# Summing modulation vectors over the partitions: a GpSimd reduction and an accumulating DMA in place of TensorE

## The chip, the cores and the metric

The kernel runs on one core of a Trainium2 chip. A core has engines that each work through their own instruction queue and wait for one another by semaphores: TensorE (PE in the profile, with its weight loads as PEld), VectorE (DVE), ScalarE (ACT), GpSimd (POOL) and SyncE (SP), which here issues most of the DMAs. The metric is the device time of one execution in microseconds (us), lower is better.

## The reference, cut to what matters

Two layers work on 256 latent and 256 context tokens of width 1024. Each layer is a half-step FFN, a mixer (neighbourhood attention in layer 0, a short convolution in layer 1) and a second half-step FFN. Around each of them the tokens are scaled, shifted and gated by modulation vectors, nine for each layer (shift, scale and gate for each of the three sub-layers); the context has its own.

```python
def half_step_ffn(x, shift, scale, gate, w_in, w_out, g, b):
    y = swiglu_ffn(modulate(x, shift, scale), w_in, w_out)
    return post_norm_update(x, y, gate, 0.5, g, b)
...
    s_c = jax.nn.silu(c)
    s_cc = jax.nn.silu(c_ctx)
    for i in range(DEPTH):
...
        m = (s_c @ ada_w[i] + ada_b[i]).reshape(B, N_MOD, 1, D)
        mc = (s_cc @ ada_w[i] + ada_b[i]).reshape(N_MOD, D)
```

The change is about the two lines for `m` and `mc`: a vector of 1024 times a matrix of 1024 x 9216, plus a bias. `m[:, 2]` is the gate of the first FFN, `m[:, 3]` and `m[:, 4]` shift and scale of the mixer, and so on.

## The kernel before, in words

**The matmuls.** All operands are float32. For TensorE each is split into a high part in the fp32r format and a low part that holds the rest, and each product is three matmuls: high by high, high by low, low by high. A weight goes this way: SP loads it to a raw tile (`w1r`, `w2r`; L205), ScalarE writes the high part (`w1h`; L210), VectorE subtracts it from the raw tile for the low part (`w1l`; L213, both inputs in SBUF), and TensorE multiplies (L679 in the first FFN, L164, L165 and L167 elsewhere). The activations between the two GEMMs of an FFN are split in the same way: `gh` by ScalarE, `gl` by VectorE (L113), from the gate product `sil` (L689). Every kind of tile has a few buffers, and a load waits until VectorE and ScalarE have read the buffer's last content.

**The first FFN** goes in three parts (`parts`, over the hidden columns). Each part is an input GEMM into `f` and an output GEMM from `gh` and `gl`; the output GEMM's results are multiplied by the gate and added to the tokens.

**The modulation vectors** come in two ways. Shift and scale of the first FFN are computed ahead of it. All other vectors, nineteen of 1024 numbers, come from the background generator `ada` (L275 to L332). The kernel's loops call `tick`, which runs a step of this generator at a given rate (0.45 steps a tick, 0.6 from the third group on), so that its instructions are queued among those of the GEMMs. A group has two vectors (the last has one):

- for each of eight row blocks `k`, SP loads a tile `ar` of 128 x 1024 weights (L303, three buffers), and VectorE multiplies it by column `k` of silu(c) and adds it onto the vector's `acc`, 128 x 1024, in two halves (L294 for the first `k`, a product only; L296 for the others). `acc` has two buffers, one for each vector of a group;
- three steps that issue nothing pass;
- what remains is the sum over the 128 partitions. TensorE multiplies `acc` by a tile of ones (L327, two halves a vector, so four matmuls a group, float32), VectorE adds the bias rows `adab` to the result `ada` in PSUM and writes `adar` (L328), and SP writes that to `scr` in DRAM (L330). The bias rows had been loaded by SP (L318) to a tile that POOL zeroed (L315).

In groups 1 to 3 the two vectors are the latents' and the context's of the same modulation, so they share their `ar` tiles: each tile is added onto both. In the later groups the two vectors have different weights, and the second `acc` is first written when the first one's eight tiles are done.

The first stream (L717) has seven groups and runs from about 80 us to the end of the first FFN. Group 1 makes the gates of the first FFN, which SP loads back from `scr` and broadcasts to all partitions after the first third (L743, `gate`). Groups 2 and 3 make shift and scale of the mixer, which `fold_cols` (L355) loads and transposes. Groups 8 to 10 follow in later phases (L1111, L1114, L1176).

POOL has little else to do: the constants at the start, two tiny operations in each layer norm (`rs`, L402 and L403), and the `bias` of the attention (L883).

Of the kernel before, what the change touches and what calls it, by code (L numbers as in the profile page):

```python
# [8 lines left out]

F32 = mybir.dt.float32  # L10
F32R = mybir.dt.float32r
AF = mybir.ActivationFunctionType
ALU = mybir.AluOpType
# [3 lines left out]
P = 128  # L17
D = 1024
# [52 lines left out]
def backbone_kernel(  # L71
# [6 lines left out]
    nc = tc.nc  # L78
    sync = nc.sync
    cp = ctx.enter_context(tc.tile_pool(name="cp", bufs=1))  # L80
# [7 lines left out]
    hp = phase.__enter__()  # L88
# [6 lines left out]
    def nm(s):  # L95
        uid[0] += 1
        return f"{s}_{uid[0]}"
# [4 lines left out]
    def bank(tag, s):  # L102
        return pp.tile([P, 512], F32, tag=tag, bufs=PB[tag], name=nm(s))
# [4 lines left out]
    def tpb(s="tp"):  # L108
        return bank("tp", s)
# [122 lines left out]

    sm.tile([P, PAD], F32, tag="fill", name="fill")
    win_sb = cp.tile([P, 64], F32, tag="wmask", name="wmask")
    ones = cp.tile([P, 32], F32, tag="ones", name="ones")
# [7 lines left out]
    warm = cp.tile([1, 1], F32, tag="warm", name="warm")  # L243
# [16 lines left out]
    nc.vector.memset(ones, 1.0)  # L260
# [11 lines left out]
    bias_rows = []  # L272
    gate_ins = []

    def ada(vecs):  # L275


        acc = {}

        def accumulate(l, m, k, w):  # L280
            with ExitStack() as st:
                for i in gate_ins:
                    st.enter_context(tc.issue_after(i.ins))
                for i, vec in enumerate(vecs):
                    if vec[:2] != (l, m):
                        continue
                    if k == 0:
                        a = hp.tile([P, D], F32, tag="acc", bufs=2, name=nm("acc"))
                        acc[i] = [a[:, 0:512], a[:, 512:D]]
                    sc = cst[:, k, vec[2]:vec[2] + 1]  # L290
                    for h in range(2):
                        src, a = w[:, h * 512:(h + 1) * 512], acc[i][h]
                        if k == 0:
                            nc.vector.tensor_scalar(a, src, sc, None, op0=ALU.mult)  # L294
                        else:
                            nc.vector.scalar_tensor_tensor(out=a, in0=src, scalar=sc, in1=a,  # L296
                                                           op0=ALU.mult, op1=ALU.add)

        loaded = []
        for l, m in dict.fromkeys((l, m) for l, m, _ in vecs):  # L300
            for k in range(KC):
                w = hp.tile([P, D], F32, tag="ar", bufs=3, name=nm("ar"))
                sync.dma_start(w, ada_w[l, k * P:(k + 1) * P, m * D:(m + 1) * D])  # L303
# [12 lines left out]
        bt = bias_rows[0]  # L316
        for i, (l, m, v) in enumerate(vecs):
            sync.dma_start(bt[64 * i:64 * i + 64:32], ada_b[l, m * D:(m + 1) * D].rearrange("(a b) -> a b", b=512))  # L318
        yield 1
        yield 1  # L320
        yield 1
        rows = hp.tile([P, 512], F32, tag="adar", name=nm("adar"))
        ps = tpb("ada")
        for i in range(len(vecs)):
            for h in range(2):
                j = 2 * i + h
                nc.tensor.matmul(ps[32 * j:32 * j + 32, :], ones, acc[i][h], start=True, stop=True)  # L327
        nc.vector.tensor_tensor(out=rows[:32 * n], in0=ps[:32 * n], in1=bt[:32 * n], op=ALU.add)  # L328
        for i, (l, m, v) in enumerate(vecs):
            sync.dma_start(scr[l][v, m * D:(m + 1) * D].rearrange("(a b) -> a b", b=512),  # L330
                           rows[64 * i:64 * i + 64:32, :])
        yield 1  # L332

    made = [0]

    def stream(*groups):
        for g in groups:
# [130 lines left out]
    def run(gen):  # L468
        for _ in gen:
            pass  # L470
# [555 lines left out]
    hp = phase.__enter__()  # L1026
# [35 lines left out]
    for i in range(len(steps) + LAG + V_LAG):  # L1062
# [14 lines left out]
        n = int(credit)  # L1077
# [12 lines left out]
        j = i - LAG - V_LAG  # L1090
# [14 lines left out]
    hTs, later = box  # L1105
    phase = tc.tile_pool(name="ph2", bufs=1)
    hp = phase.__enter__()
    bias_rows.clear()
# [19 lines left out]
    w = sc_w_in[0]  # L1128
# [45 lines left out]
    g, hTs, later = sub_end(sc_w_out[0], lhs_T(yT), KC, 1, 1, 5, 1.0, (1, 6), "wo", order_late(KU))  # L1174
# [57 lines left out]
```

## Time and profile before

| | |
|---|---|
| time, median of 3 runs | 1262.65 us (1261.54 to 1262.88) |
| span of the profiled execution | 1259.9 us |
| TensorE busy | 1245.4 us, 99% |
| VectorE busy | 952.5 us, 76% |
| ScalarE busy | 589.9 us, 47% |
| GpSimd busy | 41.4 us, 3% |
| HBM read, written | 265.27 MB, 2.17 MB |

The profiled execution has no time of its own beside its span, which lies 2.75 us under the median of the runs. The profile is one execution of the program as the hardware profiler recorded it. A row of a timeline has the start, the duration, the engine, the line, the operation, output<-inputs, and how many instructions are joined in the row; brackets at its end hold the idle time before it and what ended that. Matmuls are pipelined: a duration overlaps the next one's, so what a matmul costs is read from the distance between starts. A row of a group has the count, the busy time, the mean (or the smallest, median and largest) duration in ns, and the idle time of the engine ahead of the group's instructions. A row of the waits reads: waiting engine, line, what it waited for, us in total, times, longest.

### The profile page before, as it was taken

The numbers are of one execution on the slowest core, as the hardware profiler recorded it, in microseconds if no ns is written. First come the engines' busy times: TensorE is split into PE (matmuls) and PEld (weight loads), VectorE is DVE, ScalarE is ACT, GpSimd is POOL, SyncE is SP. The second block draws the span as 40 slices with busy tenths as digits, with TensorE's granted clock in tenths as the row PEclk, the third lists the DMA queues.
The fourth block names the chain that finished last, engine by engine and source line by source line (L and its number), as shares of the span: only waits on it lengthen the run. The fifth ranks groups of instructions, "written<-read, shape, count | busy, mean of one in ns | idle before, by whom it ended". The sixth has DMA issues, their size and how long they took to land.

```text
span 1259.9 us, 17303 instructions
## 1 busy us (share of the span) xinstructions
PE 1245.4 (99%) x5922; PEld 1007.2 (80%) x5922; DVE 952.5 (76%) x1678; ACT 589.9 (47%) x1152; POOL 41.4 (3%) x71
## 2 busy tenths in 40 slices
PE   9999999999999999999999999999999999999997
PEld 6787778777878877877888788888788887888786
DVE  3699987888878877889898546988546788876546
ACT  2432132312326456687655435655435644655431
POOL 0000000000001011121000000000000000000000
PEclk9999999999999999999999999999999999999999
DMA  9976678878842744465899645898645764886641
GB/s 300 310 241 215 197 239 280 269 255 266 300 149 85 217 93 92 93 130 170 256 342 318 225 144 169 285 340 268 214 145 170 247 202 131 262 289 184 223 158 55
DMA packets 202776, 268.59 MB, mean 213 GB/s; under 512 B 30090, under 2 KB 149362, under 8 KB 202688
## 3 DMA queue, kind: packets, MB, share of 16 engines
q1 hardware_dynamic: 202652, 267.48, 67.3%
q8 instruction: 46, 0.75, 0.2%
q14 instruction: 42, 0.34, 0.1%
q10 hardware_dynamic: 36, 0.02, 0.0%
HBM read 265.27 MB, written 2.17 MB: 212 GB/s over the span
## 4 chain that ended last, share of the span: by engine, by line
PE 92%; DVE 3%; ACT 3%; issue 1%; DMA 0%; POOL 0%; DVEq 0%; SPq 0%; ACTq 0%; POOLq 0%
PE f L679 19%; PE w L164 17%; PE w L167 17%; PE w L165 17%; PE wkv L164 2%; PE wkv L165 2%; PE wkv L167 2%; PE wc L164 2%; PE wc L167 2%; PE wc L165 2%; PE gT L487 1%; PE ada L608 1%; PE ada L327 1%; PE S L971 1%; ACT pr L979 1%
## 5 line engine op out<-in xcount | busy, mean ns | idle before, releaser
L210 ACT ACTIVATE w1h<-w1r 128x512 fp32r<-128x512 f32 (+1 forms) x352 | 199.8, 620 | 180.4 <-DMA w1r<-in_ffn_w_in_dram 73.3
L213 DVE TENSOR_TENSOR w1l<-w1r,w1h 128x512 fp32r<-128x512 f32 (+1 forms) x352 | 222.9, 679 | 44.6 <-ACT w1h L210 43.3
L164 PE MATMUL w<-w1h,hTh 128*128 128x512 f32 x528 | 209.4, 397 | 0.9 <-ACT hTh L112 0.9
L165 PE MATMUL w<-w1l,hTh 128*128 128x512 f32 x528 | 206.0, 390 | 0.2 <-DVE w1l L213 0.2
L296 DVE SCALAR_TENSOR_TENSOR acc<-ar,cst,acc 128x512 f32<-128x512 f32 x266 | 186.0, 746 | 15.4 <-DMA ar<-in_ada_w_dram 15.4
L164 PE MATMUL w<-w2h,gh 128*128 128x512 f32 (+1 forms) x446 | 173.4, 389 | 0.0
L165 PE MATMUL w<-w2l,gh 128*128 128x512 f32 (+1 forms) x446 | 172.1, 386 | 0.0
L213 DVE TENSOR_TENSOR w2l<-w2r,w2h 128x512 fp32r<-128x512 f32 x176 | 114.3, 688 | 76.0 <-ACT w2h L210 75.2
L210 ACT ACTIVATE w2h<-w2r 128x512 fp32r<-128x512 f32 x176 | 101.6, 624 | 146.0 <-PE w L167 103.6
L167 PE MATMUL w<-w1h,hTl 128*128 128x512 f32 x528 | 163.2, 390 | 0.3 <-DVE hTl L113 0.2
L167 PE MATMUL w<-w2h,gl 128*128 128x512 f32 (+1 forms) x446 | 136.1, 386 | 0.0
L679 PE MATMUL f<-h0h,w1h 128*128 128x512 f32 x352 | 133.3, 394 | 0.4 <-DVE h0h L634 0.4
L679 PE MATMUL f<-h0l,w1h 128*128 128x512 f32 x352 | 133.2, 391 | 0.0
L679 PE MATMUL f<-h0h,w1l 128*128 128x512 f32 x352 | 132.7, 390 | 0.0
L164 PEld LDWEIGHTS w<-w1h,hTh 128*128 128x128 f32 x528 | 99.2, 188 | 23.8 <-ACT hTh L112 1.7
L167 PEld LDWEIGHTS w<-w1h,hTl 128*128 128x128 f32 x528 | 98.9, 188 | 22.4 <-DVE hTl L113 1.5
L165 PEld LDWEIGHTS w<-w1l,hTh 128*128 128x128 f32 x528 | 99.2, 188 | 20.2 <-DVE w1l L213 0.6
L164 PEld LDWEIGHTS w<-w2h,gh 128*128 128x128 f32 x446 | 83.8, 188 | 19.2 <-issue 1.7
L165 PEld LDWEIGHTS w<-w2l,gh 128*128 128x128 f32 x446 | 83.8, 188 | 16.6
L167 PEld LDWEIGHTS w<-w2h,gl 128*128 128x128 f32 x446 | 83.3, 188 | 17.1
L679 PEld LDWEIGHTS f<-h0h,w1h 128*128 128x128 f32 x352 | 65.9, 189 | 18.8 <-issue 4.2
L679 PEld LDWEIGHTS f<-h0l,w1h 128*128 128x128 f32 x352 | 65.6, 188 | 14.3 <-issue 0.6
(186 smaller groups left out, 1684.5 us busy)
## 6 DMA issues: line engine op xcount, KB each, us to landing
w1r<-in_ffn_w_in_dram SPq DMA_DIRECT2D x340, 256.0 KB
ar<-in_ada_w_dram SPq DMA_DIRECT2D x128, 512.0 KB
w2r<-in_ffn_w_out_dram SPq DMA_DIRECT2D x88, 512.0 KB
ar<-in_ada_w_dram SPq DMA_DIRECT2D x32, 256.0 KB
wkvr<-in_na_w_qkv_dram SPq DMA_DIRECT2D x32, 256.0 KB
wcr<-in_sc_w_in_dram SPq DMA_DIRECT2D x32, 256.0 KB
wqr<-in_na_w_qkv_dram SPq DMA_DIRECT2D x8, 512.0 KB
wor<-in_na_w_out_dram SPq DMA_DIRECT2D x8, 512.0 KB
```

Source lines behind the costliest of these rows:

```text
L164: nc.tensor.matmul(ps, lh, rh, start=first and i == 0, stop=False)
L165: nc.tensor.matmul(ps, lh, rl, start=False, stop=False)
L167: nc.tensor.matmul(ps, ll, rh, start=False, stop=last and i == n - 1)
L210: nc.scalar.activation(hi[:, a:a + m // W_HI], raw[:, a:a + m // W_HI], AF.Copy)
L213: nc.vector.tensor_tensor(out=lo[:, a:b], in0=raw[:, a:b], in1=hi[:, a:b].bitcast(F32), op=ALU.subtract)
L296: nc.vector.scalar_tensor_tensor(out=a, in0=src, scalar=sc, in1=a, op0=ALU.mult, op1=ALU.add)
L327: nc.tensor.matmul(ps[32 * j:32 * j + 32, :], ones, acc[i][h], start=True, stop=True)
L487: nc.tensor.transpose(ps[:, j * 256 + i * P:j * 256 + (i + 1) * P], g[:, j * P:(j + 1) * P], ident)
L608: nc.tensor.matmul(ps[o:o + 32, 0:m], cst[:, a * kt + i, :], w[:, i, j, :], start=(a == 0 and i < 2), stop=(a == last and i >= kt - 2))
L679: nc.tensor.matmul(ps, w, hT0[k][part == 1], start=(k == part == 0), stop=(k == KC - 1 and part == 1))
L971: nc.tensor.matmul(banks[i], (qh, qh, ql)[f][ps, qs], (kh, kl, kh)[f][ps, :], start=f == 0, stop=f == 2)
L979: nc.scalar.activation(pr, S, AF.Exp, bias=mx[:, 0:1], accum_out=mx[:, 1:2])
```

## The change

The multiplication of `ar` by silu(c) and its accumulation on VectorE stay. The sum over the partitions is made by POOL: `partition_all_reduce`, a library instruction, reads `acc` (128 x 1024) and writes the sum to all partitions of a new tile `red`, which has one buffer. A DMA on POOL's queue then adds row 0 of `red` onto `scr` in DRAM. So that the bias is in the sum, three DMAs of SP copy `ada_b` to `scr` beforehand. The tile of ones, the bias rows, the matmuls of L327, the addition of L328 and the writes of L330 are gone. Where a group's end took four steps of the generator, it takes one. After a stream's last reduction a tiny POOL operation on `warm` follows it.

```diff
-                        a = hp.tile([P, D], F32, tag="acc", bufs=2, name=nm("acc"))
-                        acc[i] = [a[:, 0:512], a[:, 512:D]]
+                        acc[i] = hp.tile([P, D], F32, tag="acc", bufs=2, name=nm("acc"))
...
+        def summed(i):
+            l, m, v = vecs[i]
+            red = hp.tile([P, D], F32, tag="red", name=nm("red"))
+            nc.gpsimd.partition_all_reduce(red, acc[i], P, ReduceOp.add)
+            nc.gpsimd.dma_start(scr[l][v:v + 1, m * D:(m + 1) * D], red[0:1], accum_op=ALU.add)
+            if i == len(vecs) - 1 and made[0] + 1 == groups[0]:
+                nc.gpsimd.tensor_tensor(out=warm, in0=red[0:1, 0:1], in1=lnc[0:1, 0:1], op=ALU.add)
...
-        n = 2 * len(vecs)
-        if not bias_rows:
-            bias_rows.append(hp.tile([P, 512], F32, tag="adab", name=nm("adab")))
-            nc.gpsimd.memset(bias_rows[0], 0.0)
-        bt = bias_rows[0]
-        for i, (l, m, v) in enumerate(vecs):
-            sync.dma_start(bt[64 * i:64 * i + 64:32], ada_b[l, m * D:(m + 1) * D].rearrange("(a b) -> a b", b=512))
+        for i in range(len(vecs)):
+            summed(i)
         yield 1
-        yield 1
-        yield 1
-        rows = hp.tile([P, 512], F32, tag="adar", name=nm("adar"))
-        ps = tpb("ada")
-        for i in range(len(vecs)):
-            for h in range(2):
-                j = 2 * i + h
-                nc.tensor.matmul(ps[32 * j:32 * j + 32, :], ones, acc[i][h], start=True, stop=True)
-        nc.vector.tensor_tensor(out=rows[:32 * n], in0=ps[:32 * n], in1=bt[:32 * n], op=ALU.add)
-        for i, (l, m, v) in enumerate(vecs):
-            sync.dma_start(scr[l][v, m * D:(m + 1) * D].rearrange("(a b) -> a b", b=512),
-                           rows[64 * i:64 * i + 64:32, :])
-        yield 1
...
     sync.dma_start(win_sb, win_mask)
+    for l, v in ((0, 0), (0, 1), (1, 0)):
+        sync.dma_start(scr[l][v].rearrange("(a b) -> a b", a=16), ada_b[l].rearrange("(a b) -> a b", a=16))
     sync.dma_start(rope, rope_tab.rearrange("(t p) a b -> p t a b", p=P))
```

The order in which the instructions stand is set by the generator's steps, so it moves as well. In the rows that follow, `acc`, `ar`, `w1r`, `w1h`, `w1l`, `sil`, `f` and `gl` are the tiles named above with the numbers of their buffers; a wait on Pool, PE, DVE or Activation is one on that engine, one on DMAHW is one on a DMA that SP or ACT issued, one on DMASW one that POOL issued. Lines are those of the kernel named: L293 and L291 after the change are L296 and L294 before it, L214 is L213, L678 is L689, L114 is L113, L308 is L303, L734 is L743, L206 is L205.

VectorE, at the border of groups 1 and 2, before the change:

```order
L296 SCALAR_TENSOR_TENSOR acc_711<-ar_897,cst,acc_711 128x512
L296 SCALAR_TENSOR_TENSOR acc_714<-ar_897,cst,acc_714 128x512 [waits DVE_49] x2
L213 TENSOR_TENSOR w1l_1033<-w1r_1031,w1h_1032 128x512 [waits DMAHW7_49,DMAHW2_49]
L213 TENSOR_TENSOR w1l_1042<-w1r_1040,w1h_1041 128x512 [waits DMAHW1_49,DMAHW0_49]
L213 TENSOR_TENSOR w1l_1033<-w1r_1031,w1h_1032 128x512
L213 TENSOR_TENSOR w1l_1042<-w1r_1040,w1h_1041 128x512
L689 TENSOR_TENSOR sil_157_944<-sil_157_944,f_155_915 128x512 [waits PE_49,Activation_49]
L113 TENSOR_TENSOR gl_948<-sil_157_944,gh_947 128x512 [waits Activation_49]
L294 TENSOR_SCALAR acc_994<-ar_992,cst 128x512 [waits DMAHW6_49,PE_49]
L328 TENSOR_TENSOR adar_970<-ada_971,adab_922 128x512 [waits DMAHW4_49,PE_49]
```

VectorE at the same border after the change:

```order
L293 SCALAR_TENSOR_TENSOR acc_712<-ar_898,cst,acc_712 128x512 [waits DVE_49]
L293 SCALAR_TENSOR_TENSOR acc_715<-ar_898,cst,acc_715 128x512 [waits DVE_49] x2
L291 TENSOR_SCALAR acc_943<-ar_941,cst 128x512 [waits DMAHW1_49,Pool_49]
L291 TENSOR_SCALAR acc_943<-ar_941,cst 128x512
L214 TENSOR_TENSOR w1l_1054<-w1r_1052,w1h_1053 128x512 [waits DMAHW5_49,DMAHW3_49]
L293 SCALAR_TENSOR_TENSOR acc_943<-ar_969,cst,acc_943 128x512 [waits DMAHW2_49,DVE_49]
L293 SCALAR_TENSOR_TENSOR acc_943<-ar_969,cst,acc_943 128x512 [waits DVE_49]
L214 TENSOR_TENSOR w1l_1045<-w1r_1043,w1h_1044 128x512 [waits DMAHW4_49]
L214 TENSOR_TENSOR w1l_1054<-w1r_1052,w1h_1053 128x512
L678 TENSOR_TENSOR sil_161_955<-sil_161_955,f_155_916 128x512 [waits PE_49,Activation_49]
L291 TENSOR_SCALAR acc_946<-ar_941,cst 128x512 [waits Pool_49]
```

The next group's first product now stands directly behind the last accumulate of the group before, where six instructions of other work lay between, and it waits for POOL where it waited for TensorE; its second vector's first product waits for POOL again, six rows on. The bias addition is gone.

POOL, from the constants to the second group, before and after. `ISA` is a library load where it has no operands, and the reduction where it has them.

```order
L315 MEMSET adab_922 128x512
masks.py:199 ISA
masks.py:199 AFFINE_SELECT ident<-ident 128x128 [waits Pool_49]
L402 TENSOR_TENSOR rs_3345<-mv_3343,lnc 128x1 [waits DVE_49,Pool_49]
L403 TENSOR_TENSOR rs_3345<-rs_3345,lnc 128x1 [waits Pool_49]
```

And after:

```order
masks.py:199 AFFINE_SELECT ident<-ident 128x128 [waits Pool_49]
L299 ISA
L299 ISA red_923<-acc_712 128x1024 [waits DVE_49]
L300 DMA scr_114<-red_923 16x1x64 [waits DMAHW0_49,Pool_49]
L299 ISA red_926<-acc_715 128x1024 [waits DMASW0_49,DVE_49]
L300 DMA scr_114<-red_926 16x1x64 [waits DMAHW3_49,Pool_49]
L299 ISA red_1155<-acc_943 128x1024 [waits DMASW1_49,DVE_49]
L300 DMA scr_114<-red_1155 16x1x64 [waits Pool_49]
```

Each reduction waits for its `acc` on VectorE and for the landing of the DMA before it, which reads the one buffer of `red`. The `rs` operations come behind the first stream's reductions.

SP, where the first gate is loaded, after the change:

```order
L308 DMA ar_987<-in_ada_w_dram 128x1024 [waits DMAHW6_49,DMAHW3_49,DVE_49]
L734 DMA gate_1136<-scr_114 128x1024 [waits DMAHW4_49,DMASW0_49]
L206 DMA w2r_1175<-in_ffn_w_out_dram 128x2x512 [waits DMAHW5_49,DVE_49,Activation_49]
L308 DMA ar_1006<-in_ada_w_dram 128x1024 [waits DMAHW1_49,DVE_49]
L308 DMA ar_1030<-in_ada_w_dram 128x1024 [waits DMAHW7_49,DMAHW2_49,DVE_49]
```

The two writes of L330 that stood ahead of the gate load are gone; the gate load waits for POOL's first accumulating DMA instead, and a load of `w2r` and further loads of `ar` stand behind it. On TensorE nothing moves but that the 38 `ada` matmuls are gone.

More of the change, by code (lines that the diff above doesn't have):

```diff
@@ L6 @@
 from concourse import mybir
+from concourse.bass_isa import ReduceOp
 from concourse.masks import make_identity
@@ L234, in backbone_kernel @@
     win_sb = cp.tile([P, 64], F32, tag="wmask", name="wmask")
-    ones = cp.tile([P, 32], F32, tag="ones", name="ones")
     ident = cp.tile([P, P], F32, tag="ident", name="ident")
@@ L259, in backbone_kernel @@
     nc.scalar.activation(cst[:, :, 0:2], pt[:, 0:16].rearrange("p (v k) -> p k v", v=2), AF.Silu)
-    nc.vector.memset(ones, 1.0)
     sel = cp.tile([P, 4], F32, tag="sel", name="sel")
@@ L269, in backbone_kernel @@
     xscr = tc.dram_tile([2 * P, D], F32, name="xscr")
-    bias_rows = []
     gate_ins = []
@@ L287, in accumulate @@
                     if k == 0:
-                        a = hp.tile([P, D], F32, tag="acc", bufs=2, name=nm("acc"))
-                        acc[i] = [a[:, 0:512], a[:, 512:D]]
+                        acc[i] = hp.tile([P, D], F32, tag="acc", bufs=2, name=nm("acc"))
                     sc = cst[:, k, vec[2]:vec[2] + 1]
                     for h in range(2):
-                        src, a = w[:, h * 512:(h + 1) * 512], acc[i][h]
+                        src, a = w[:, h * 512:(h + 1) * 512], acc[i][:, h * 512:(h + 1) * 512]
                         if k == 0:
@@ L311, in ada, with stream @@
                 yield 1
-        n = 2 * len(vecs)
-        if not bias_rows:
-            bias_rows.append(hp.tile([P, 512], F32, tag="adab", name=nm("adab")))
-            nc.gpsimd.memset(bias_rows[0], 0.0)
-        bt = bias_rows[0]
-        for i, (l, m, v) in enumerate(vecs):
-            sync.dma_start(bt[64 * i:64 * i + 64:32], ada_b[l, m * D:(m + 1) * D].rearrange("(a b) -> a b", b=512))
-        yield 1
-        yield 1
-        yield 1
-        rows = hp.tile([P, 512], F32, tag="adar", name=nm("adar"))
-        ps = tpb("ada")
-        for i in range(len(vecs)):
-            for h in range(2):
-                j = 2 * i + h
-                nc.tensor.matmul(ps[32 * j:32 * j + 32, :], ones, acc[i][h], start=True, stop=True)
-        nc.vector.tensor_tensor(out=rows[:32 * n], in0=ps[:32 * n], in1=bt[:32 * n], op=ALU.add)
-        for i, (l, m, v) in enumerate(vecs):
-            sync.dma_start(scr[l][v, m * D:(m + 1) * D].rearrange("(a b) -> a b", b=512),
-                           rows[64 * i:64 * i + 64:32, :])
+        for i in range(len(vecs)):
+            summed(i)
         yield 1
     made = [0]
-    def stream(*groups):
-        for g in groups:
+    groups = [0]
+    def stream(*vecs):
+        groups[0] = made[0] + len(vecs)
+        for g in vecs:
             yield from ada(g)
@@ L1107, in backbone_kernel @@
     hp = phase.__enter__()
-    bias_rows.clear()
     ext[0] = 3
```

## The prediction, made before the changed kernel ran

> **What bounds the kernel now.** I read the page first: span, busy shares, slices and the chain of waits.
>
> ```profile
> span 1259.9 us, 17303 instructions
> ...
> PE 1245.4 (99%) x5922; PEld 1007.2 (80%) x5922; DVE 952.5 (76%) x1678; ACT 589.9 (47%) x1152; POOL 41.4 (3%) x71
> ...
> PE   9999999999999999999999999999999999999997
> ...
> DVE  3699987888878877889898546988546788876546
> ...
> PE 92%; DVE 3%; ACT 3%; issue 1%; DMA 0%; POOL 0%; DVEq 0%; SPq 0%; ACTq 0%; POOLq 0%
> ```
>
> TensorE is full in every slice but the last and is 92% of the chain: whatever takes matmuls away shortens the kernel, whatever makes TensorE wait lengthens it. Next, TensorE's waits: of those on the split weights this is the largest row.
>
> ```profile
> PE w L165 <- DVE w1l L213: 0.2, 1, 0.2
> ```
>
> So VectorE, whose `w1l`, `w2l` and `gl` feed every matmul group, is in time today. How much room has it? The windows answer, VectorE alone: from the background's start to the end of the first output GEMM, then to the end of the first stream, then on.
>
> ```profile
> core 0: us, DVE busy (x), PEclk, DMA share, GB/s
> 80.00:160.00 80.00, 72.20 (x117) 1.00 0.67 212
> 160.00:315.00 155.00, 126.50 (x201) 1.00 0.81 262
> 315.00:366.00 51.00, 41.77 (x67) 1.00 0.79 266
> ```
>
> It idles 80.00 - 72.20 = 7.8 us in the first stretch and 28.5 us in the second. That is thin, and just there run seven of the ten groups that the change rewrites. The clock is full throughout and moves no term.
>
> **What is removed.** On TensorE, four `ada` matmuls a group. The timeline at group 1:
>
> ```profile
> 96.30 0.39 PE L679 MATMUL f<-h0h,w1l 128*128 128x512 f32 x1
> 96.53 0.39 PE L679 MATMUL f<-h0l,w1h 128*128 128x512 f32 x1
> ...
> 96.85 1.07 PE L327 MATMUL ada<-acc,ones 128*32 128x512 f32 x8
> 97.84 0.50 PE L679 MATMUL f<-h0h,w1h 128*128 128x512 f32 x1
> ```
>
> Neighbours start 0.23 us apart (96.30, 96.53), but the next useful one comes at 97.84: 1.31 - 0.23 = 1.08 us. Ten groups: **-10.9 us**, on the path. VectorE loses ten bias adds.
>
> ```profile
> L328 DVE TENSOR_TENSOR adar<-ada,adab x10: 675/684/686, 98.4 to 1181.1; 128x512 f32<-128x512 f32 x9, 64x512 f32<-64x512 f32 x1
> ```
>
> At about 0.6 us of net relief each I take 1.2 us for the two that stood ahead of the output GEMM's end (160.4), and 3.0 us for five ahead of 313.9. SP loses 38 small DMAs and gains three prefills, 110 KB in all, among the first weight loads. Its queue waits for VectorE to free buffers, not for its own issues, so I count nothing for either.
>
> ```profile
> SPq L303 <- DVE acc L296: 155.8, 102, 6.4
> ```
>
> If that cover were gone, it would be 38 issues of about half a microsecond (1.02 us for two, in a row below), 19 us of SP's time gained.
>
> **What is moved.** Four background steps at a group's end become one, so each later group starts three steps sooner. Counted in the order, ahead of the first splits for the second third of the FFN (matmuls from 160.41) stand 100 accumulates, where there were 80; ahead of the four splits at 313.91 all 224, where there were 192.
>
> ```profile
> 100.16 2.07 DVE L296 SCALAR_TENSOR_TENSOR acc<-ar,cst,acc 128x512 f32<-128x512 f32 x3
> ...
> 98.98 1.27 DVE L294 TENSOR_SCALAR acc<-ar,cst 128x512 f32<-128x512 f32 x3
> ...
> 160.41 0.39 PE L679 MATMUL f<-h0h,w1h 128*128 128x512 f32 x1
> ...
> 313.91 2.50 DVE L213 TENSOR_TENSOR w1l<-w1r,w1h 128x512 fp32r<-128x512 f32 x4 [0.31 <-ACT w1h L210]
> ```
>
> At 2.07/3 = 0.69 us each that is 20 x 0.69 = 13.8 us earlier VectorE work by 160, and 32 x 0.69 = 22.1 us by 314.
>
> **What is added.** Nineteen partition reductions on POOL, whose time R no row has. The nearest rows are an elementwise POOL operation and POOL's first other work:
>
> ```profile
> L883 POOL TENSOR_TENSOR bias<-bias,wmask 128x256 f32<-128x256 f32 x28 | 22.4, 801 | 128.1 <-DMA bias<-in_na_rpb_dram 119.7 <-DVE pT L113 6.7 <-DVE mx L977 1.6
> ...
> 385.99 0.19 POOL L402 TENSOR_TENSOR rs<-mv,lnc 128x1 f32<-128x1 f32 x1 [384.14 <-DVE mv L400]
> ```
>
> One pass over 128x1024 is four of 128x256: 4 x 0.80 = 3.2 us, the lower end. Seven halving passes (128 = 2^7), each at full cost, are 22.4 us, the upper. Nothing lies nearer to one than to the other, so I take the geometric middle, **R = 8.5 us**, as an estimate. POOL itself has room: nothing until 386, so also the library loads are covered there (uncovered, they would sit ahead of a group's first reduction and add to its border below).
>
> Then the accumulating DMA, D. Today's pair of small writes and the load that waits for it:
>
> ```profile
> 99.09 1.02 SPq L330 DMA_DIRECT2D scr<-adar  x2
> ...
> 100.77 0.35 SPq L743 DMA_DIRECT2D gate<-scr  x1
> ```
>
> From 99.09 to 100.77, 1.7 us; read-and-add may take up to three times that. I take 2. `red` has one buffer, so each reduction waits for the DMA before it. In SP's queue the first gate load now waits for such a DMA, with a `w2r` load behind it: once, at most R + D = 10.5 us. I count nothing, since before that load others are already under way; if TensorE needs that one next, it is up to 10.5.
>
> **The new wait.** `acc` has two buffers. In groups 1 to 3 both vectors share each weight tile, so both are in use to the end, and the next group's first product waits for POOL. By the order, between the end of the first `acc` (when its reduction starts) and the second wait stand: two accumulates (1.4), two products (1.27/3 = 0.42 each, 0.8), three weight splits and two accumulates (5 x 0.69 = 3.4), one gate product (estimated 0.7): 6.3 us. At borders 1 and 2 the waits therefore come to 2R + D - 6.3 = 12.7 us each. At border 3 only one `acc` is wanted soon: R - 1.4 = 7.1 us. Sum 32.5 us. Behind the waiting instruction in VectorE's queue stand splits of `w1r` and `gl`, and for those TensorE waits. At later borders some 16 accumulates and the splits among them lie between last use and reuse: no wait at this R.
>
> **Does a running reduction hold up VectorE?** Around the `bias` operations of POOL:
>
> ```profile
> 412.80 2.44 DVE L213 TENSOR_TENSOR wkvl<-wkvr,wkvh 128x512 fp32r<-128x512 f32 x3
> ...
> 413.90 0.79 POOL L883 TENSOR_TENSOR bias<-bias,wmask 128x256 f32<-128x256 f32 x1 [10.34 <-DMA bias<-in_na_rpb_dram]
> ...
> 415.17 1.28 DVE L113 TENSOR_TENSOR qTl<-qT,qTh 128x512 fp32r<-128x512 f32 x2
> ...
> 416.13 0.74 POOL L883 TENSOR_TENSOR bias<-bias,wmask 128x256 f32<-128x256 f32 x1 [1.43 <-DMA bias<-in_na_rpb_dram]
> ...
> 416.36 1.05 DVE L213 TENSOR_TENSOR wkvl<-wkvr,wkvh 128x512 fp32r<-128x512 f32 x1
> ...
> L213 DVE TENSOR_TENSOR w1l<-w1r,w1h 128x512 fp32r<-128x512 f32 (+1 forms) x352 | 222.9, 679 | 44.6 <-ACT w1h L210 43.3
> ...
> L296 DVE SCALAR_TENSOR_TENSOR acc<-ar,cst,acc 128x512 f32<-128x512 f32 x266 | 186.0, 746 | 15.4 <-DMA ar<-in_ada_w_dram 15.4
> ```
>
> A split takes 0.68 us (679 ns); the one that began at 416.36 under a running POOL operation took 1.05 and ended at 417.41, 0.54 after POOL did (416.13 + 0.74 = 416.87). It stood still while POOL ran. The three from 412.80 lost 2.44 - 3 x 0.68 = 0.4 us in the same way. `qTl`, of which one input is in PSUM, took 0.64 each: not held. The splits and the accumulates both read two SBUF operands. So if a reduction holds VectorE as this operation does, VectorE loses R at every reduction, needed soon or not.
>
> The Trainium skill states this as a rule ("SBUF — State Buffer", section "Who interferes with whom"): a VectorE instruction with two SBUF inputs and a GpSimd instruction that reads SBUF share a port pair, and the first to get it blocks the other for its whole instruction. The trace agrees for the 0.79 us operation; for a library instruction nothing here shows it. By that rule the sum is the first below, without it the second.
>
> **The sums**, as TensorE's delay, at the span of 1259.9; the median of the runs is 1262.65, 2.75 above, and I add the change to the median.
> - Held. By 313.9, 13 reductions: 13 x 8.5 = 110.5, and 22.1 pulled forward, less 36.3 idle and 3.0 saved: 93.3; this covers the border waits, since VectorE stands still either way. Less 10.9: +82.4. For the last five reductions,
>
> ```profile
> 600.00:780.00 180.00, 180.00 (x821) 147.66 (x821) 130.46 (x222) 90.42 (x173) 1.08 (x2) 1.00 0.75 248
> ```
>
> the third busy figure is VectorE's: 49.5 of 180 us idle, so most is absorbed: between 0 and 42.5, I take 5. +87, **1350 us**.
> - Not held. By 160: 32.5 + 13.8 - 7.8 - 1.2 = 37.3, less 10.9: +26.4, 1289, say **1290 us**.
>
> **Rivals and chances.** A difference of 0.2%, 2.5 us, is about what a measurement of this kernel can tell.
> - Held, R near 8.5: **0.45**, forecast 1350. R from 6.5 to 11 moves it by 13 x 2 to 2.5, hence its own range 1318 to 1385.
> - Not held, only the borders wait: **0.25**, 1290. For it: a library instruction may read SBUF in pieces. Against: the rows at 413.90 and 416.13.
> - Long reduction, R of 12 to 22 us: **0.13**. Unheld, the borders cost 5R + 2D - 14: at R = 12, 50 us, so 1307; held, 13 x 22.4 gives above 1500. A page of the Trainium skill ("GPSIMD Engine Reference", section 3.2 "Cross-partition — where GPSIMD wins") has 247,699 ns for a partition-axis reduction of 128x2048; half would be an estimated 124 us for each of ours, and the kernel would be milliseconds long. No run here shows that; the POOL rows speak for far less.
> - Same: **0.05**. R = 3.2 unheld: borders 2 x 2.1 + 1.8 = 6.0, plus 13.8 - 7.8 - 1.2 makes 10.8, against 10.9 gained: 1263.
> - Faster: **0.12**. The three borders cease to wait: if R is under about 3 us and VectorE isn't held, `acc` is free again within the 6.3 us of other work, only pulled-forward work is left, 13.8 - 9.0 = 4.8 us or less, and TensorE keeps 6 to 10.9 us: 1252 to 1257, say 1256. It decides from a sum of border waits under 6 us, the same case's. For it speaks that TensorE waits for a split only 0.2 us today; against it that one pass alone costs 3.2 us.
>
> The number is the likeliest case's. The range runs from 1262, which leaves out the faster case, to 1420, which leaves out the long half of the held long reductions. Faster 0.12, same 0.05, slower 0.83.
>
> **What would show it.** The `ada` matmuls gone and their gaps closed. The group of the 19 reductions gives R: 6.5 to 11 for the forecast. Held: means of the accumulates and of the `w1l` splits well over 746 and 679 ns between 90 and 330 us, with single ones of several us that end just after a reduction; unheld: these means as before, and VectorE's waits on POOL ahead of the first products at three borders. Either way TensorE's waits on `w1l`, `w2l` and `gl` rise from under 1 us to tens, before 330 us. Wrong if R is under 3 us, if the split's mean is unchanged and TensorE doesn't wait, or if the time is lost after 400 us or in SP's queue behind the gate load.

## The result and the profile after

The changed kernel takes 1322.99 us (median of 4 runs, 1322.0 to 1325.18) against 1262.12 us of the kernel before on the same chips: ratio 1.0485, interval 1.047 to 1.05, so 60.9 us slower. The forecast was 1350, with 1262 to 1420 as its range and 1318 to 1385 as the likeliest case's own.

The page of the changed kernel: span, busy times, TensorE's slices, the clock, the chain.

```profile
span 1321.7 us, 17202 instructions
...
PE 1255.5 (95%) x5846; PEld 1014.7 (77%) x5846; DVE 1008.8 (76%) x1667; ACT 588.1 (44%) x1152; POOL 190.7 (14%) x111
...
PE   8997769897899999999999999999999999999997
...
PEclk9998889898999999999999999999999999999999
...
PE 62%; DVE 15%; issue 10%; DMA 6%; ACT 3%; POOL 3%; SPq 0%; DVEq 0%; ACTq 0%; POOLq 0%
```

The clock row of the kernel before:

```profile
PEclk9999999999999999999999999999999999999999
```

The damage is all in slices 4 to 11 (a slice is 33 us: 99 to 364 us). The first stream's fourteen reductions start between 89 and 375 us. Behind them TensorE is full again. VectorE and POOL have come into the chain. Unforeseen: TensorE's busy time grew by 10 us though 76 matmul records are gone, and TensorE's granted clock (`PEclk`, in tenths of full speed), 9 or more everywhere before, drops to 8 in five of these eight slices.

The groups of `w1l` splits, reductions and accumulates, from the same page:

```profile
L214 DVE TENSOR_TENSOR w1l<-w1r,w1h 128x512 fp32r<-128x512 f32 (+1 forms) x352 | 245.4, 746 | 40.7 <-ACT w1h L211 39.9
...
L299 POOL PARTITION_ALL_REDUCE red<-acc x19 | 132.3, 6964 | 514.8 <-DVE acc L293 509.0
...
L293 DVE SCALAR_TENSOR_TENSOR acc<-ar,cst,acc 128x512 f32<-128x512 f32 x266 | 194.3, 778 | 11.4 <-DMA ar<-in_ada_w_dram 11.4
```

R is 6.96 us on average (8.5 taken). The splits' mean went from 679 to 746 ns, the accumulates' from 746 to 778. The products, a group's first operation on each half of `acc`, changed most; their smallest, median and largest durations in ns, before and after:

```profile
L294 DVE TENSOR_SCALAR acc<-ar,cst x38: 475/480/491, 53.8 to 1081.2; 128x512 f32<-128x512 f32 x38
```

```profile
L291 DVE TENSOR_SCALAR acc<-ar,cst x38: 473/486/4761, 59.9 to 1143.5; 128x512 f32<-128x512 f32 x38
```

All three groups are many undisturbed instructions and a few very long ones. One such, with the reduction that runs beside it (POOL's row) on VectorE's timeline:

```profile
140.62 6.11 POOL L299 PARTITION_ALL_REDUCE red<-acc  x1 [1.77 <-DMA scr<-red]
140.78 4.91 DVE L293 SCALAR_TENSOR_TENSOR acc<-ar,cst,acc 128x512 f32<-128x512 f32 x1
145.61 0.68 DVE L380 SCALAR_TENSOR_TENSOR x<-x,res 128x512 f32<-128x512 f32 x1
```

An accumulate of 0.75 us took 4.91. It ended at 145.69, which is 1.04 us before the reduction's own end (146.73). The same figure of 1.03 to 1.05 us comes back at every held split and accumulate. So a reduction holds such instructions until its last microsecond, at most some 4.3 us of delay for one of them. Of the fourteen reductions, four hold an accumulate or a split (16.5 us in all), seven hold products (31 us), and during the first three VectorE waits for POOL. A held product ends 1.30 us before the reduction; where a second one follows, it ends 0.28 us after the reduction.

VectorE's waits on POOL, and TensorE's on the split weights and `gl`:

```profile
PE f L668 <- DVE w1l L214: 19.4, 6, 8.8
...
DVE acc L291 <- POOL red L299: 18.4, 5, 6.0
...
PE w L166 <- DVE w2l L214: 13.8, 6, 8.3
...
PE f L668 <- ACT w1h L211: 7.8, 4, 3.9
...
PE w L168 <- DVE gl L114: 4.9, 2, 4.6
```

Both mechanisms of the forecast are there: waits at borders, and TensorE waiting for splits (0.2 us before). The three long waits on POOL are those of the first products of groups 2 (two vectors) and 3, on VectorE:

```profile
96.42 0.88 DVE L291 TENSOR_SCALAR acc<-ar,cst 128x512 f32<-128x512 f32 x2 [6.03 <-POOL red L299]
...
106.45 0.88 DVE L291 TENSOR_SCALAR acc<-ar,cst 128x512 f32<-128x512 f32 x2 [5.42 <-POOL red L299]
...
137.81 0.88 DVE L291 TENSOR_SCALAR acc<-ar,cst 128x512 f32<-128x512 f32 x2 [5.41 <-POOL red L299]
```

Last, what TensorE does after such a wait. Its timeline:

```profile
139.34 0.79 PE L168 MATMUL w<-w2h,gl 128*128 128x512 f32 x1 [4.59 <-DVE gl L114]
139.93 0.63 PE L165 MATMUL w<-w2h,gh 128*128 128x512 f32 x1
140.36 0.63 PE L166 MATMUL w<-w2l,gh 128*128 128x512 f32 x1
...
144.20 1.05 PE L168 MATMUL w<-w2h,gl 128*128 128x512 f32 x2
145.05 0.46 PE L165 MATMUL w<-w2h,gh 128*128 128x512 f32 x1
145.36 0.39 PE L166 MATMUL w<-w2l,gh 128*128 128x512 f32 x1
145.59 0.39 PE L165 MATMUL w<-w2h,gh 128*128 128x512 f32 x1
```

And the windows, TensorE alone; the column behind its busy time is the granted clock:

```profile
core 0: us, PE busy (x), PEclk, DMA share, GB/s
139.40:145.00 5.60, 5.60 (x13) 0.50 0.05 1
145.10:155.00 9.90, 9.90 (x45) 1.00 0.49 129
```

After a wait of 4.59 us the starts lie 0.43 us apart for 5.7 us, at a granted clock of 0.50, then 0.23 again, at 1.00. So a long wait is paid a second time, in slow matmuls. Worked out from all neighbouring starts between 80 and 400 us: gaps over 0.6 us sum to 53.5 us beyond the pitch (before: 7.6, the seven `ada` holes), and the slower pitch in between to about 18 us (before: about 1). Of these 18 us some 15 stand behind the eight gaps of over 3 us, two of which have a gap of 0.73 us right behind them; the other ten gaps, up to 2.1 us, have 0.9 us behind them at most. Together TensorE lost about 63 us more than before in this stretch, less 1.2 us saved at each of the groups 8 to 10: 59 of the 60.9 us.

### The profile page after: what moved, and what is told of

Same layout as the page of the kernel before. It is cut to its first block, busy times and chain, and to the rows that moved or that the text cites. A ratio compares the mean times of both kernels' runs of the same rounds, so it can differ in the third digit from the quotient of the medians.

```text
span 1321.7 us, 17202 instructions
## 1 busy us (share of the span) xinstructions
PE 1255.5 (95%) x5846; PEld 1014.7 (77%) x5846; DVE 1008.8 (76%) x1667; ACT 588.1 (44%) x1152; POOL 190.7 (14%) x111
## 4 chain that ended last, share of the span: by engine, by line
PE 62%; DVE 15%; issue 10%; DMA 6%; ACT 3%; POOL 3%; SPq 0%; DVEq 0%; ACTq 0%; POOLq 0%
PE w L168 13%; PE w L165 13%; PE w L166 13%; PE f L668 5%; DVE acc L293 5%; DVE w1l L214 3%; DMA w1r<-in_ffn_w_in_dram 3%; POOL red L299 3%; DMA ar<-in_ada_w_dram 3%; PE wkv L165 2%; PE wkv L166 2%; PE wkv L168 2%; PE wc L165 2%; PE wc L168 2%; PE wc L166 2%
## 5 line engine op out<-in xcount | busy, mean ns | idle before, releaser
L214 DVE TENSOR_TENSOR w1l<-w1r,w1h 128x512 fp32r<-128x512 f32 (+1 forms) x352 | 245.4, 746 | 40.7 <-ACT w1h L211 39.9
L299 POOL PARTITION_ALL_REDUCE red<-acc x19 | 132.3, 6964 | 514.8 <-DVE acc L293 509.0
L293 DVE SCALAR_TENSOR_TENSOR acc<-ar,cst,acc 128x512 f32<-128x512 f32 x266 | 194.3, 778 | 11.4 <-DMA ar<-in_ada_w_dram 11.4
L166 PE MATMUL w<-w2l,gh 128*128 128x512 f32 (+1 forms) x446 | 175.5, 394 | 13.8 <-DVE w2l L214 13.8
L214 DVE TENSOR_TENSOR w2l<-w2r,w2h 128x512 fp32r<-128x512 f32 x176 | 113.9, 688 | 73.8 <-ACT w2h L211 73.0
L668 PE MATMUL f<-h0h,w1l 128*128 128x512 f32 x352 | 138.0, 405 | 19.4 <-DVE w1l L214 19.4
L668 PE MATMUL f<-h0h,w1h 128*128 128x512 f32 x352 | 137.1, 405 | 8.2 <-ACT w1h L211 7.8
L168 PE MATMUL w<-w2h,gl 128*128 128x512 f32 (+1 forms) x446 | 138.9, 392 | 4.9 <-DVE gl L114 4.9
L668 PE MATMUL f<-h0l,w1h 128*128 128x512 f32 x352 | 137.2, 403 | 0.0
L165 PEld LDWEIGHTS w<-w2h,gh 128*128 128x128 f32 x446 | 85.0, 191 | 22.1 <-ACT gh L113 5.2
L668 PEld LDWEIGHTS f<-h0h,w1l 128*128 128x128 f32 x352 | 68.6, 195 | 36.7 <-DVE w1l L214 22.4
```

What stands on the lines that cost most here:

```text
L165: nc.tensor.matmul(ps, lh, rh, start=first and i == 0, stop=False)
L166: nc.tensor.matmul(ps, lh, rl, start=False, stop=False)
L168: nc.tensor.matmul(ps, ll, rh, start=False, stop=last and i == n - 1)
L214: nc.vector.tensor_tensor(out=lo[:, a:b], in0=raw[:, a:b], in1=hi[:, a:b].bitcast(F32), op=ALU.subtract)
L299: nc.gpsimd.partition_all_reduce(red, acc[i], P, ReduceOp.add)
L668: nc.tensor.matmul(ps, w, hT0[k][part == 1], start=(k == part == 0), stop=(k == KC - 1 and part == 1))
```

## The experiments

The theory after these readings has three parts: a running reduction holds VectorE; the first products wait at borders; groups pulled forward crowd VectorE. All ratios below are to the kernel before, run beside each experiment (1261.6 to 1261.9 us).

**The steps put back.** The empty steps stand behind the reductions.

```diff
         for i in range(len(vecs)):
             summed(i)
         yield 1
+        yield 1
+        yield 1
+        yield 1
```

> The changed kernel with the three empty steps of the generator put back behind a group's reductions, so that the next group starts as late as before. Theory (three parts: reductions hold VectorE some 4 us each, the first products wait for POOL at three borders, and later groups are pulled forward): the waits of about 18 us and most of the 22 us pulled forward go, the holds stay: 1275 to 1295 us. Rival one (only borders and pulled-forward work cost anything): about 1252 us, under the kernel before. Rival two (the holds alone cost): 1315 us or more.

Measured: 1322.16 us, ratio 1.0478 (1.0464 to 1.0493), like the changed kernel. The edit did less than I meant. VectorE's order is made by priorities, and ahead of the 49th weight split there stand 76 accumulates and products, where the kernel before has 64 and the changed one 80. The products still waited for POOL:

```profile
DVE acc L291 <- POOL red L299: 20.2, 3, 7.3
```

So this run says nothing on what the borders or the order cost, though the time falls in rival two's range.

**A third `acc`.** The reduction writes in place, and nobody has to wait at a border.

```diff
-                        acc[i] = hp.tile([P, D], F32, tag="acc", bufs=2, name=nm("acc"))
+                        acc[i] = hp.tile([P, D], F32, tag="acc", bufs=3, name=nm("acc"))
...
-            red = hp.tile([P, D], F32, tag="red", name=nm("red"))
+            red = acc[i]
```

> The changed kernel with three acc buffers instead of two, the reduction writing in place (no tile red, for room). VectorE's waits on POOL at the first borders should fall from 18 us to under 8; the pulled-forward accumulates stay. Theory of three parts: some of the waits come back as holds, because VectorE now has an accumulate to run while the reduction runs: 1300 to 1318 us. Rival (the waits at the borders carry the loss): under 1285 us.

Measured: 1322.68 us, ratio 1.0483 (1.0467 to 1.05). The products have no wait on a reduction left, but instead:

```profile
L293 DVE SCALAR_TENSOR_TENSOR acc<-ar,cst,acc 128x512 f32<-128x512 f32 x266 | 203.7, 812 | 9.8 <-DMA ar<-in_ada_w_dram 9.6
...
L291 DVE TENSOR_SCALAR acc<-ar,cst 128x512 f32<-128x512 f32 x38 | 57.5, 1546 | 7.6 <-DMA ar<-in_ada_w_dram 4.9 <-DMA scr<-acc 2.7
```

The accumulates' mean rose from 778 to 812 ns and the products take 1546. Summed over the first fourteen reductions, VectorE's instructions ran 61.4 us over their medians, where in the changed kernel it was 47.7 us and 18.4 us of waits, 66.1 together. The border waits can be had away, and VectorE stands still under the reductions instead: the rival, that the borders carry the loss, falls, and so does my own lower figure of 1300 to 1318.

**Fills in place of the reduction.**

```diff
-            nc.gpsimd.partition_all_reduce(red, acc[i], P, ReduceOp.add)
+            nc.gpsimd.tensor_tensor(out=warm, in0=acc[i][0:1, 0:1], in1=acc[i][0:1, 512:513], op=ALU.add)
+            for _ in range(6):
+                nc.gpsimd.memset(red, 0.0)
+            nc.gpsimd.tensor_tensor(out=warm, in0=acc[i][0:1, 1:2], in1=acc[i][0:1, 513:514], op=ALU.add)
```

> The changed kernel with the reduction replaced by POOL work of about the same length that reads next to nothing from SBUF: a tiny read of acc, six fills of red with zeros (about 6.5 us), a tiny read of acc. The sums over the partitions are left out (scr gets the bias alone). The order of the instructions stays as in the changed kernel. Theory of three parts: borders and pulled-forward work cost as before, the holds on accumulates and splits go (some 40 us of stretched VectorE instructions in the first FFN): 1275 to 1295 us. Rival (it is the borders and the order alone): 1315 to 1325 us. Rival (holds alone): about 1255 us.

Measured: 1274.31 us, ratio 1.0101 (1.0087 to 1.0115). The accumulates and splits are back at 745 and 679 ns. But the fills don't depend on `acc`, and POOL ran them ahead; its two reads then came together, `acc` was free at once and the waits on POOL fell to 5.9 us. So the run took away the holds and most of the border waits as well: both together are worth 48.7 us, and which of them was left to the next runs.

**The reduction beside the kernel before.** For room, this kernel and its control have 36 activation tiles, not 38. TensorE still sums; POOL reduces a constant tile, `spare`, that nobody reads.

```diff
-NACT = 38
+NACT = 36
...
+        for i in range(len(vecs)):
+            nc.gpsimd.tensor_tensor(out=spare[0:1, 0:1], in0=acc[i][0][0:1, 0:1], in1=acc[i][1][0:1, 0:1], op=ALU.add)
+            nc.gpsimd.partition_all_reduce(spare, spare, P, ReduceOp.add)
         yield 1
         yield 1
         yield 1
         rows = hp.tile([P, 512], F32, tag="adar", name=nm("adar"))
```

> The kernel before with 36 activation tiles instead of 38, which makes room for the tile of e4_beside: the control of that run. Both theories: 1262 us, or a few us more if the two tiles were needed.

> The kernel before with 36 activation tiles, TensorE still summing, order and steps as before. Beside it POOL reduces a constant tile of 128x1024 in place, nineteen times, each started by a tiny read of an acc that is complete; nobody waits for the result, and acc is free as soon as TensorE has read it. Theory (a running reduction holds VectorE some 4 us): 14 holds of about 4.2 us in the first FFN are 59 us, less 36 us of idle time there: 20 to 35 us above the control. Rival (only waits for the reduction's result and the changed order cost): within 3 us of the control.

Measured: control 1261.68 us, ratio 1.0001 (0.9992 to 1.001); with the reductions 1306.82 us, ratio 1.0354 (1.034 to 1.0369): 45.1 us for reductions whose result nobody waits for. The group rows, and VectorE's one wait on this work:

```profile
L299 DVE SCALAR_TENSOR_TENSOR acc<-ar,cst,acc 128x512 f32<-128x512 f32 x266 | 218.8, 865 | 9.0 <-DMA ar<-in_ada_w_dram 8.9
...
L324 POOL PARTITION_ALL_REDUCE spare<-spare x19 | 124.6, 6556 | 143.5 <-issue 120.0 <-DVE sil L695 10.0 <-DVE acc L299 6.8
```

```profile
DVE acc L297 <- POOL spare L323: 8.6, 2, 5.2
```

A group's second tiny read stands behind its first reduction, so `acc` came free late at two places, 8.6 us. Even if all of that was lost, 36 of the 45 us are holds and what follows from them, in the order of the kernel before. Over the first fourteen reductions VectorE's instructions ran 59.1 us over their medians, as expected. Of these 67.7 us of holds and waits about 36 were absorbed, as credited: TensorE's gaps, read as above but to the end of the first FFN, grew by 31.3 us (7.6 in the control, 38.9 here). Another 9.5 us is slow matmuls (1.9 in the control, 11.4 here), which I had not counted.

**Fills beside the kernel before.** The same kernel with write-only work, which here does wait for the tiny read.

```diff
-            nc.gpsimd.partition_all_reduce(spare, spare, P, ReduceOp.add)
+            for _ in range(6):
+                nc.gpsimd.memset(spare, 0.0)
```

> As e4_beside, but what POOL does beside the kernel before is write only: each tiny read of a complete acc is followed by six fills of the spare tile with zeros, about 6 us. If a POOL operation holds VectorE's accumulates and splits because it reads SBUF, these run at their 746 and 685 ns: within 5 us of the control's 1261.7. Rival (any POOL work of that length does it): 1295 to 1310 us, as e4_beside had 1306.8.

Measured: 1263.39 us, ratio 1.0012 (1.0003 to 1.0022).

```profile
L214 DVE TENSOR_TENSOR w1l<-w1r,w1h 128x512 fp32r<-128x512 f32 (+1 forms) x352 | 222.4, 677 | 44.6 <-ACT w1h L211 42.8
...
L299 DVE SCALAR_TENSOR_TENSOR acc<-ar,cst,acc 128x512 f32<-128x512 f32 x266 | 185.6, 743 | 10.7 <-DMA ar<-in_ada_w_dram 10.5
...
L297 DVE TENSOR_SCALAR acc<-ar,cst 128x512 f32<-128x512 f32 x38 | 25.9, 716 | 7.0 <-PE ada L334 5.3 <-DMA ar<-in_ada_w_dram 1.7
```

Splits and accumulates run at their old times: the 25 accumulates and 54 splits that ran while a fill did took at most 753 and 694 ns. So it is not any POOL work that holds them, but something that the reduction does and a fill doesn't. That this is its reading of SBUF fits the POOL `bias` operations of the kernel before, which read SBUF and held a split (416.36 us in the prediction); no run parts the reduction's reads from the rest of what it does. The products are slower under fills too, 716 ns on average.

**No reduction at all.** Row 0 of `acc` goes to DRAM as it is, so the sums over the partitions are left out. What stays is the order, the wait for the DMA, and TensorE's saving.

```diff
-            red = hp.tile([P, D], F32, tag="red", name=nm("red"))
-            nc.gpsimd.partition_all_reduce(red, acc[i], P, ReduceOp.add)
+            red = acc[i]
...
-            if i == len(vecs) - 1 and made[0] + 1 == groups[0]:
-                nc.gpsimd.tensor_tensor(out=warm, in0=red[0:1, 0:1], in1=lnc[0:1, 0:1], op=ALU.add)
```

> The changed kernel without its reductions: the accumulating DMA reads row 0 of acc directly, so the sums over the partitions are left out. What is left is the changed order (later groups start earlier), the wait for the DMA at the borders (2 to 5 us), and TensorE's saving of 12 us. If the earlier order costs what the prediction gave it (13.8 to 22 us less VectorE's idle time), about 1262 to 1275 us, as e3_memset had 1274. Rival (the order costs nothing, the fills of e3_memset did): 1250 to 1254 us.

Measured: 1267.34 us, ratio 1.0043 (1.0026 to 1.0059): 5.7 us above the kernel before. With TensorE's saving as the run with groups 8 to 10 on POOL gives it (1.22 us a group, 12.2 for ten) the earlier order and the DMAs cost 17.9 us. VectorE waited only 0.6 us for a DMA out of `acc`, so at the borders the DMAs cost little; what they may have delayed in SP's queue was not told apart from the order. The reductions are then 1322.99 - 1267.34, about 55.6 us.

**Half the columns.** Reduction and DMA over the first 512 columns; the other half of each vector keeps its bias alone.

```diff
-            nc.gpsimd.partition_all_reduce(red, acc[i], P, ReduceOp.add)
-            nc.gpsimd.dma_start(scr[l][v:v + 1, m * D:(m + 1) * D], red[0:1], accum_op=ALU.add)
+            nc.gpsimd.partition_all_reduce(red[:, 0:512], acc[i][:, 0:512], P, ReduceOp.add)
+            nc.gpsimd.dma_start(scr[l][v:v + 1, m * D:m * D + 512], red[0:1, 0:512], accum_op=ALU.add)
```

> The changed kernel with each reduction and its DMA over the first 512 columns alone; the other half of every vector keeps only its bias, so half of the sums are left out. If a reduction's time and its hold grow with the columns, R is about 3.3 us and a hold about 2.1 us, and half of the 48 us between the changed kernel and e3_memset goes: 1290 to 1303 us. Rival (a fixed cost for each call): R over 5 us, 1312 us or more.

Measured: 1293.22 us, ratio 1.0245 (1.0231 to 1.0259). An undisturbed reduction takes 3.23 us instead of 6.11, and the longest hold is 2.0 us instead of 4.3. Both grow with the columns, with little fixed cost, and 29.8 of the 55.6 us go with half of the work.

**POOL for groups 8 to 10 alone.** TensorE keeps the first seven groups. `full[i]` is the whole `acc` of a vector.

```diff
+        if made[0] >= 7:
+            for i, (l, m, v) in enumerate(vecs):
+                red = hp.tile([P, D], F32, tag="red", name=nm("red"))
+                nc.gpsimd.partition_all_reduce(red, full[i], P, ReduceOp.add)
+                nc.gpsimd.dma_start(scr[l][v:v + 1, m * D:(m + 1) * D], red[0:1], accum_op=ALU.add)
...
+            yield 1
+            return
         n = 2 * len(vecs)
```

> The kernel before, with POOL's reduction and the accumulating DMA for groups 8 to 10 alone (the five vectors behind the first FFN), TensorE for the first seven. In the changed kernel's trace TensorE gains 1.1 to 1.2 us at each of these three groups and loses nothing: 1258.5 us, 3.6 below the kernel before. Rival (holds of VectorE cost anywhere they fall): 1262 or above.

Measured: 1258.23 us, ratio 0.9969 (0.9958 to 0.998): 3.7 us faster than the kernel before, the best of all. Each group on POOL saves 1.22 us here, so ten would save 12.2. It is not that VectorE isn't held; the last reduction, VectorE's and POOL's rows:

```profile
1145.10 6.83 DVE L214 TENSOR_TENSOR w1l<-w1r,w1h 128x512 fp32r<-128x512 f32 x4
1145.33 6.46 POOL L317 PARTITION_ALL_REDUCE red<-acc  x1 [78.86 <-DVE acc L298]
1151.86 0.68 DVE L114 TENSOR_TENSOR gl<-gT,gh 128x512 fp32r<-128x512 f32 x1
```

Four splits take 6.83 us instead of 2.5, but one 4.3 us hold at a time is covered by the weights that lie ready there, and TensorE doesn't wait.

**Group 7 on POOL as well**, the last of the first FFN, in place.

```diff
-        if made[0] >= 7:
+        if made[0] >= 6:
...
-                red = hp.tile([P, D], F32, tag="red", name=nm("red"))
+                red = full[i]
```

> As e5_hybrid, with group 7, the last of the first FFN, on POOL as well (reduced in place, no tile red). If VectorE has time there, TensorE gains 1.2 us more: 1257.0 us. If VectorE hasn't, two holds of 4 us and the group that is done three steps sooner cost up to 8 us: 1258 to 1266 us.

Measured: 1262.85 us, ratio 1.0011 (1.0002 to 1.0019), 4.6 us more than without group 7. The group's second reduction meets the first FFN's last activations:

```profile
357.21 6.40 POOL L317 PARTITION_ALL_REDUCE acc<-acc  x1 [15.90 <-PE f L690]
...
358.92 3.65 DVE L114 TENSOR_TENSOR gl<-sil,gh 128x512 fp32r<-128x512 f32 x1 [0.70 <-ACT gh L113]
```

`gl`, which reads `sil` and `gh` in SBUF, takes 3.65 us instead of 0.69. The next gate product is late, and its `gh` is what TensorE then waits for:

```profile
367.50 0.50 PE L165 MATMUL w<-w2h,gh 128*128 128x512 f32 x1 [1.92 <-ACT gh L113]
```

Two reductions in a tight stretch cost more than TensorE's hole.

## Why the prediction was right, step by step

- **TensorE's saving.** Right, slightly small: 1.22 us a group against 1.08, 12.2 against 10.9 us. Kept in full only from group 8 on.
- **R.** Right in kind, large in size: a mean of 6.96 us, 6.11 where nothing disturbs, against an estimated 8.5; inside the 6.5 to 11 that the forecast asked for. With 6.96 the forecast's own sum gives 1330. (Its range of 1318 to 1385 is wider than its working: 13 x 2 and 13 x 2.5 from 1350 are 1324 and 1382.5.) R lies nearer to the lower row (four elementwise passes, 3.2 us) than to seven passes.
- **Held, or not.** Right, and the step on which all hung: the likeliest case, not the unheld one, and shown by two runs that differ in it and in the library loads of the reductions (45.1 us with reductions beside the kernel before, 1.7 with fills). Its reason, two SBUF inputs, is a part of it: accumulates and splits are held, but in the changed kernel 31 of the 47.7 us fell on products, which have one SBUF input and of whose being held it said nothing. The size was off as well: an instruction is held until about a microsecond before the reduction's end and the hold was 3.0 to 4.3 us, not R. For all fourteen it summed to 47.7 us, with 18.4 us of waits where VectorE had nothing else to do: 66.1 us, where the sum had 110.5 for thirteen.
- **The border waits.** Right in place: 11.5 us at border 1, 5.9 at border 2 and 1.1 at border 3, 18.4 against 32.5. R was shorter, and D was 2.1 to 4.8 us (median 3.9) against 2. "Covered, since VectorE stands still either way" was right: with the third `acc` the time did not change.
- **Idle time as a credit.** 36.3 us of VectorE's idle time and 3.0 of saved adds were set against the holds and the work pulled forward. Where holds are long this nearly came out: 66.1 + 22.1 - 36.3 - 3.0 = 48.9 us of waits for TensorE, and its gaps are 53.5. Beside the kernel before it came out to the figure: 59.1 + 8.6 - 36.3 = 31.4, and the gaps grew by 31.3. Where there are none it failed: pulled forward without holds should have cost at most 4.8 us; TensorE's gaps were 10.3, the slow matmuls behind them some 6 more, and the order and the DMAs together cost 17.9. That VectorE's idle time doesn't lie where the earlier work falls is likely, but was not shown.
- **The slow matmuls after a wait.** Missing from the sum: "the clock moves no term" was true of the kernel before only. 17 us, a quarter of what TensorE lost in the first FFN.
- **The last five reductions.** 5 us taken, none lost, as shown by the run with groups 8 to 10 on POOL.

Holds (with the border waits) that were taken 44 us too large for the first stream, and 5 us for the last five reductions, stand against 17 us of slow matmuls that were left out and some 5 us of credit that didn't come. So the sum came out 27 us too high and no more: the mechanism was right in the main, and that the number is as near as it is owes something to luck, since errors of 49 and 22 us offset each other in part.

Of the rivals: "not held" is out by the fills. "Faster" is out since its condition, R under 3 us, isn't met; without any reduction the kernel is still 5.7 us slower. The long reduction is out too: the Trainium skill's 247,699 ns for a partition-axis reduction of 128x2048 ("GPSIMD Engine Reference", section 3.2 "Cross-partition — where GPSIMD wins") is for another operation, and half of it is eighteen times the 6.96 us measured here. The Trainium skill's rule of the shared port ("SBUF — State Buffer", section "Who interferes with whom") bore out for the library instruction in the main: instructions with two SBUF inputs are held by the reduction, which reads SBUF, and not by fills, which only write; but the hold ends 1.03 to 1.05 us before the reduction does, not with it. The library loads and the gate load behind POOL's DMA were both counted at nothing. The gate load kept SP's queue waiting for 8.5 us; but TensorE's first wait in this stretch ends on a split that VectorE ran late, behind its waits for POOL, and no wait was traced to either.

## What to carry to other kernels

An idle engine is not free if its work can hold the engine that feeds the bottleneck: ask what a long POOL instruction does in SBUF, and which VectorE instructions lie beside it; here those with two SBUF inputs were held, and products with one as well. Put such work where the feeder has a lead (groups 8 to 10: 3.7 us won) and not where it runs just in time (groups 1 to 7: about 64 us lost). Before crediting an engine's idle share against work that is moved forward, look at where the idle time lies; and reckon with a second price on TensorE, in slow matmuls, behind many waits of some microseconds.

## What the runs showed that I had not expected

A hold seems to go both ways. While VectorE issues splits back to back, these run at full pace and the reduction takes longer; rows of POOL and VectorE in the changed kernel:

```profile
184.59 9.55 POOL L299 PARTITION_ALL_REDUCE red<-acc  x1 [2.41 <-DVE w1l L214]
...
185.06 3.09 DVE L214 TENSOR_TENSOR w1l<-w1r,w1h 128x512 fp32r<-128x512 f32 x5
188.07 0.68 DVE L375 SCALAR_TENSOR_TENSOR res<-w,gate 128x512 f32<-128x512 f32 x1
188.68 4.42 DVE L214 TENSOR_TENSOR w1l<-w1r,w1h 128x512 fp32r<-128x512 f32 x1
```

Five splits pass at 0.6 us each, then `res`, which reads a PSUM tile and the gate, gives the opening; the next split is held until 193.10, and the reduction took 9.55 us instead of 6.11. The reductions at 753.24 and 897.20 us show the same: three splits pass, `gl` follows, which reads the PSUM tile `gT`, the next split is held, and they take 7.68 and 7.66 us.

The products (`tensor_scalar`, one SBUF input, 0.48 us for 128x512) are held too, though they don't have two inputs: up to 4.76 us in the changed kernel, 1546 ns on average with three `acc` buffers, and 716 ns even beside fills, which leave the two-input instructions alone. The Trainium skill ("SBUF — State Buffer", section "Who interferes with whom") names `tensor_scalar` among the operations that can enter two-port modes and then contend with GpSimd; that these products ran in one was not tested.

TensorE's half pace lasted 5.7 us after a wait of 4.59 us. In the changed kernel 0.6 to 2.8 us were lost behind each gap of over 3 us. Length alone doesn't decide: with reductions beside the kernel before, a gap of 4.36 us had 0.1 us behind it and one of 2.49 us had 1.7. What else does was not tried.
